# A max-pooling kernel: a short first load from one contiguous stretch, its outputs stored in the middle of the loads

## The chip, the cores and the metric

One core of one Trainium2 chip. The metric is the device time of one execution in microseconds (us); unless a range is given, a time below is a median of 4 to 9 executions. Every execution used here is marked as fast in the record, none as slow, and the granted clock was 1.0 in all.

## The reference

`x` is float32 of shape 32 x 256 x 4096 (134.2 MB). Each row of 4096 is cut into 256 windows of 16, and the output is the maximum of each window (32 x 256 x 256, 8.4 MB).

```python
for i in range(output_size):                       # 256
    start = int(i * length / output_size)
    end = int((i + 1) * length / output_size)
    result[:, :, i] = np.max(x[:, :, start:end], axis=-1)
```

## The kernel before

All 2,097,152 windows are dealt out to 128 partitions, 16,384 to each. One SBUF area of 53,200 floats per partition holds three load slots at its low end and all outputs at its high end. Outputs grow downwards, so the three slots shrink from round to round (1024, 980, 924, ... windows). Loads and stores go through one queue, issued by SyncE; VectorE reduces each slot as it lands. The outputs are stored at the end: those of the first nine loads, those of the middle loads, and the last four loads' by themselves.

```python
    sizes = []
    left = total
    while left:
        room = AREA - (total - left)
        n = min(room // (SLOTS * W + SLOTS) // ALIGN * ALIGN, MOST)   # W = 16, MOST = 1024
        for _ in range(SLOTS):                                        # SLOTS = 3
            n = min(n, left)
            if n:
                sizes.append(n)
                left -= n
    groups = [sizes[: ROUNDS_A * SLOTS], sizes[ROUNDS_A * SLOTS :]]   # ROUNDS_A = 3
    # ... (cut)
    for g, loads in enumerate(groups):
        n = sum(loads)
        xg = xw[first : first + P * n].rearrange("(p n) w -> p (n w)", p=P)
        og = ow[first : first + P * n].rearrange("(p n) -> p n", p=P)
        first += P * n
        base = low - n
        b = n
        for i, size in enumerate(loads):
            a = b - size
            at = n_loads % SLOTS * sizes[n_loads // SLOTS * SLOTS] * W
            slot = area[:, at : at + size * W]
            nc.sync.dma_start(out=slot, in_=xg[:, a * W : b * W])
            nc.vector.reduce_max(out=area[:, base + a : base + b],
                in_=slot.rearrange("p (n w) -> p n w", w=W), axis=mybir.AxisListType.X)
            n_loads += 1
            b = a
        # ... (cut: stores of a group are put on a list)
    for dst, src in stores:
        nc.sync.dma_start(out=dst, in_=src)
```

A "row" below is one partition's share of one DMA: one contiguous run in memory and one packet on one of the 16 DMA engines. With 128 partitions, each engine moves 8 rows per DMA. The rows of a load lie one group share apart: 562,176 B in the first group, 486,400 B in the second. This distance is the pitch.

## Time and profile before

Median 335.48 us (335.36 to 335.57, 6 runs).

| | before |
|---|---|
| span of the profiled execution | 333.9 us |
| DMA queue, share of 16 engines' span | 99.1% |
| moved | 142.61 MB, 427 GB/s |
| VectorE busy | 276.0 us, 83% |
| first reduce begins | 22.98 us |
| last reduce ends | 326.0 us |

Lines of the page of the kernel before: VectorE's busy time, share and instructions, then the one DMA queue with its packets, MB and share of the 16 engines' span.

```profile
span 333.9 us, 109 instructions
DVE 276.0 (83%) x19; POOL 0.2 (0%) x4
...
q1 hardware_dynamic: 3168, 142.61, 99.1%
HBM read 134.22 MB, written 8.39 MB: 427 GB/s over the span
```

The DMA engines are the limit, VectorE is not. The timeline of the kernel before shows the same. Its columns are start us, duration us, engine, source line, operation, output and input, count; in brackets stands how long the engine had idled and for what.

```profile
22.98 17.22 DVE L75 TENSOR_REDUCE area<-area 128x1024 f32<-128x16384 f32 x1 [22.98 <-DMA area<-in_x_dram]
42.33 17.22 DVE L75 TENSOR_REDUCE area<-area 128x1024 f32<-128x16384 f32 x1 [2.13 <-DMA area<-in_x_dram]
...
293.16 33.20 SPq L91 DMA_DIRECT2D out_dram<-area  x3
...
308.79 17.21 DVE L75 TENSOR_REDUCE area<-area 128x768 f32<-128x12288 f32 x2 [1.57 <-DMA area<-in_x_dram]
```

Loads of 8.39 MB land 19.35 us apart, each is reduced in 17.22 us, and the reducer waits for the next. The last reduce ends at 326.0 us; the final store is issued then, behind two earlier stores still running.

How many packets began in the first 2.75 us, by the DMA view of that window:

```profile
DMA packets 16, 1.05 MB, mean 381 GB/s; under 512 B 0, under 2 KB 0, under 8 KB 0
```

A 64 KB row takes 2.4 us, so 16 packets here are the first row of each of the 16 engines: all have started.

Two things can be worked out from the packets in the trace. A packet takes about 14 ns plus 0.0367 ns per byte, whether load or store, from 10 KB (387 ns, median) to 64 KB (2418 ns). The main exception is the very first row of each engine, which takes 2.8 to 3.8 us. And no engine idles between its first packet and its last, in this kernel.

### The profile page before, as it was taken

To read this page: it belongs to the slowest core of one execution; us is meant where nothing else is said; L and a number is where in the kernel's file an instruction comes from. 1 tells how busy PE (TensorE), PEld (TensorE's weight loads), DVE (VectorE), ACT (ScalarE), POOL (GpSimd) and SP (SyncE) were. 2 spreads that over 40 slices of the span, in tenths; PEclk is the share of its full clock that TensorE was granted. 3 is DMA by queue.
4 is the path that set the end of the run, shared out by engine and by line. 5 is a ranking of instruction groups with operands and counts; after the bars stand their busy time and mean duration, and the time that the engine had idled before them with its cause. 6 is when DMAs were issued, how large, how long until landed. Compare 5 with 4: busy or idle time off the path is not lost.

```text
span 333.9 us, 109 instructions
## 1 busy us (share of the span) xinstructions
DVE 276.0 (83%) x19; POOL 0.2 (0%) x4
## 2 busy tenths in 40 slices
DVE  0029899798979899897979897979989798988990
POOL 0000000000000000000000000000000000000000
DMA  9898989998999998999999999999999998998997
GB/s 377 377 502 377 495 385 471 392 473 376 473 443 398 474 439 383 425 453 453 446 426 433 426 426 426 426 425 469 407 419 475 395 465 389 465 436 383 448 420 311
DMA packets 3168, 142.61 MB, mean 427 GB/s; under 512 B 352, under 2 KB 352, under 8 KB 352
## 3 DMA queue, kind: packets, MB, share of 16 engines
q1 hardware_dynamic: 3168, 142.61, 99.1%
HBM read 134.22 MB, written 8.39 MB: 427 GB/s over the span
## 4 chain that ended last, share of the span: by engine, by line
DMA 63%; DVE 34%; another core or an unknown queue 1%; issue 0%; SPq 0%
DMA area<-in_x_dram 63%; DVE area L75 34%; SPq L74 0%
## 5 line engine op out<-in xcount | busy, mean ns | idle before, releaser
L75 DVE TENSOR_REDUCE area<-area 128x1024 f32<-128x16384 f32 (+6 forms) x19 | 276.0, 14525 | 50.0 <-DMA area<-in_x_dram 50.0
L108 POOL MEMSET const-bfloat16-1.0<- 128x1 bf16 x1 | 0.1, 102 | 0.0
L108 POOL MEMSET const-uint8-127<- 128x1 uint8 x1 | 0.1, 101 | 0.0
L108 POOL MEMSET const-float32-0.0<- 128x1 f32 x1 | 0.1, 100 | 0.2 <-issue 0.2
L108 POOL MEMSET const-float32-1.0<- 128x1 f32 x1 | 0.1, 99 | 0.0
## 6 DMA issues: line engine op xcount, KB each, us to landing
area<-in_x_dram SPq DMA_DIRECT2D x3, 7840.0 KB, 39.1
area<-in_x_dram SPq DMA_DIRECT2D x3, 7392.0 KB, 36.9
area<-in_x_dram SPq DMA_DIRECT2D x3, 6944.0 KB, 34.7
area<-in_x_dram SPq DMA_DIRECT2D x3, 6528.0 KB, 32.6
area<-in_x_dram SPq DMA_DIRECT2D x3, 6144.0 KB, 30.7
out_dram<-area SPq DMA_DIRECT2D x1, 4392.0 KB, 30.7
out_dram<-area SPq DMA_DIRECT2D x1, 2526.0 KB, 36.3
area<-in_x_dram SPq DMA_DIRECT2D x1, 1952.0 KB, 20.7
```

What stands on the lines that cost most here:

```text
L75: nc.vector.reduce_max(out=area[:, base + a : base + b], in_=slot.rearrange("p (n w) -> p n w", w=W), axis=mybir.AxisListType.X,)
L108: nc = _bacc.Bacc("TRN2", target_bir_lowering=False, num_devices=1)
```

## The change

The intent, as the diff shows it: VectorE should get its first data early, by a first load of 320 windows (20 KB) per partition instead of 1024 (64 KB), read as a group of its own, so from one contiguous stretch of 2.6 MB (its rows lie back to back; "packed" below). Its outputs are stored after the ninth load, on the same queue, instead of at the end. The slots are sized again from what is left. Loads stay 19; stores become 4 instead of 3.

```diff
+    FIRST = 320
+    EARLY_AT = 9
-    sizes = []
-    left = total
+    slot_sizes = [MOST]
+    rounds = [[FIRST] + [MOST] * (SLOTS - 1)]
+    left = total - sum(rounds[0])
     while left:
         room = AREA - (total - left)
         n = min(room // (SLOTS * W + SLOTS) // ALIGN * ALIGN, MOST)
+        if left <= slot_sizes[-1]:
+            n = left
 ... (cut: rounds are filled with n)
-    groups = [sizes[: ROUNDS_A * SLOTS], sizes[ROUNDS_A * SLOTS :]]
+    groups = [sizes[:1], sizes[1 : ROUNDS_A * SLOTS], sizes[ROUNDS_A * SLOTS :]]
 ... (cut)
-            at = n_loads % SLOTS * sizes[n_loads // SLOTS * SLOTS] * W
+            at = n_loads % SLOTS * slot_sizes[n_loads // SLOTS] * W
 ... (cut)
+            if n_loads == EARLY_AT:
+                dst, src = stores.pop(0)
+                nc.sync.dma_start(out=dst, in_=src)
```

More of the change, by code (lines that the diff above doesn't have):

```diff
@@ L45 @@
         n = min(room // (SLOTS * W + SLOTS) // ALIGN * ALIGN, MOST)
-        for _ in range(SLOTS):
+        if left <= slot_sizes[-1]:
+            n = left
+        slot_sizes.append(n)
+        rounds.append([])
+        while left and len(rounds[-1]) < SLOTS:
             n = min(n, left)
-            if n:
-                sizes.append(n)
-                left -= n
-    groups = [sizes[: ROUNDS_A * SLOTS], sizes[ROUNDS_A * SLOTS :]]
+            rounds[-1].append(n)
+            left -= n
+    sizes = [n for r in rounds for n in r]
+    groups = [sizes[:1], sizes[1 : ROUNDS_A * SLOTS], sizes[ROUNDS_A * SLOTS :]]
     pool = ctx.enter_context(tc.tile_pool(name="pool", bufs=1))
@@ L81 @@
             b = a
+            if n_loads == EARLY_AT:
+                dst, src = stores.pop(0)
+                nc.sync.dma_start(out=dst, in_=src)
         low = base
-        if g == 0:
+        if g < len(groups) - 1:
             stores.append((og, area[:, base : base + n]))
```

## The prediction

> **What bounds the kernel now.** The DMA engines, from first packet to last. The page gives the DMA queue 99.1% of 16 engines' span, 142.61 MB at 427 GB/s; VectorE is busy 83%. The single packets of the trace show no gap: the 16 engines start at 1.75 to 2.03 us, run back to back, and end at 331.3 to 332.5 of a 333.9 us span. So about 1.7 us lie before the stream and 1.4 us after it; the rest is bytes. VectorE's waits in the timeline (0.85 to 2.13 us before each reduce, 23.0 before the first) are slack of an engine that doesn't bind: a 128x16384 reduce takes 17.22 us, its load 19.35.
>
> The Trainium skill ("DMA: Bandwidth & Descriptors", Specifications) gives a fabric ceiling of 435 GB/s; the trace agrees: a 64 KB row takes 2418 ns on one engine, which is 434 GB/s over 16. No rate is left to win.
>
> **What the change does, costed.**
> - Bytes: the same, one queue, still 19 loads. One store more (4), so 8 rows more per engine. Packet times by row length (10,192 B 388 ns, 35,136 B 1303, 62,720 B 2315) lie on a line of 0.0367 ns per byte plus about 14 ns per row. 8 rows cost **+0.1 us**, all on the critical path. The 164 KB store (estimate 0.5 us) only moves from the end to the middle.
> - First load 20 KB instead of 64 KB per partition: it should land at about 9.5 us instead of 23.0, and the first reduce (5.4 us) end near 15 instead of 40. This slack VectorE doesn't need; loads 2 and 3 are queued anyway. Worth 0. The first row on each engine takes 2.8 to 3.8 us instead of 2.42; that start-up latency (mean 0.9) should remain.
> - Larger slots (996 instead of 980 and so on): no effect, by the line above.
> - Tail: the last load grows from 244 to 756 outputs. It should land at about 313.5 us; its reduce takes 12.7 us instead of 4.2 (the previous reduce now ends before it lands), ending near 326.3, as before (326.0). The two stores behind the last load (4.0 and 2.6 MB, 15.3 us) keep the engines busy until 328 to 329. The final store needs about 1 us from issue to first packet, so it is ready near 327.3, some 0.6 us to spare (before: 1.4). No bubble.
>
> **Sum.** 335.48 + 0.1 = 335.6 us, range 335.1 to 336.3.
>
> **What would show it.** DMA share again 99%, no packet gaps; first reduce starting near 9.7 us; VectorE's busy time still 276 us, its waits only moved (short before the first reduce, long before the second, about 1 us before the last); the last store's packets following without a gap; packet times on the same line.
>
> **What would make it wrong.** (1) Rows of the last group lie 526,080 B apart, near 512 KiB; the Trainium skill (same page, Latency and other measured facts) reports rates falling at large power-of-two row pitches. Before, pitches of 562,176 and 486,400 B show no difference; if this one does, half of the loads slow by a few per cent. (2) The early 1,280 B writes disturb the reads around them by over 0.5 us. (3) The final store comes after the queue has run dry: up to 1 us. (4) The contiguous first load shortens the start-up: up to 1 us faster.
>
> Chances: faster by over 2% 0.01, within 2% 0.96, slower by over 2% 0.03.

## The result, and the profile after

Median 336.30 us (336.12 to 336.57, 6 runs) against 335.48: by the medians 0.82 us slower. The ratio is 1.0026, 95% interval 1.0013 to 1.0039. Such a ratio is the mean time of one kernel's fast runs over that of the other's of the same rounds, so not quite the ratio of the medians quoted. By the 2% line that is "the same"; by the interval it is a small, real loss.

The page of the changed kernel, the same lines:

```profile
span 334.7 us, 110 instructions
DVE 276.0 (82%) x19; POOL 0.2 (0%) x4
...
q1 hardware_dynamic: 3312, 142.61, 98.8%
HBM read 134.22 MB, written 8.39 MB: 426 GB/s over the span
```

The timeline of the changed kernel, the first reduces, those around the early store, and the end:

```profile
10.29 5.49 DVE L84 TENSOR_REDUCE area<-area 128x320 f32<-128x5120 f32 x1 [10.29 <-DMA area<-in_x_dram]
29.61 17.22 DVE L84 TENSOR_REDUCE area<-area 128x1024 f32<-128x16384 f32 x1 [13.84 <-DMA area<-in_x_dram]
...
140.82 15.75 DVE L84 TENSOR_REDUCE area<-area 128x936 f32<-128x14976 f32 x1 [1.88 <-DMA area<-in_x_dram]
158.81 15.75 DVE L84 TENSOR_REDUCE area<-area 128x936 f32<-128x14976 f32 x1 [2.23 <-DMA area<-in_x_dram]
...
314.75 12.75 DVE L84 TENSOR_REDUCE area<-area 128x756 f32<-128x12096 f32 x1 [1.22 <-DMA area<-in_x_dram]
327.53 0.33 SPq L103 DMA_DIRECT2D out_dram<-area  x1
```

VectorE does start 12.7 us sooner, and then waits 13.84 us for the second load. Early data is worth nothing to an engine that isn't the limit. But the first load is also late: 44 KB less per row is 8 x 1657 ns = 13.26 us less per engine (by the medians, 2418 and 761 ns), so from 22.98 the first reduce should have come to 9.72 us, and it came at 10.29. That is 0.57 us of loss before anything else has happened. The DMA view of the first 2.75 us of the changed kernel:

```profile
DMA packets 15, 0.31 MB, mean 112 GB/s; under 512 B 0, under 2 KB 0, under 8 KB 0
```

15 packets, not 16: one engine has not started. The single packets show it starting at 2.95 us (in the kernel before the last engine starts at 2.03), and then taking 0.91 us beyond the line for its first row. No engine started its second row in this window, so the 15 are 15 engines.

Why one engine of 16 counts: the Trainium skill ("DMA: Bandwidth & Descriptors", section "Why a DMA increments its semaphore by 16 and not by 1") says that the participating engines finish independently and only the full count means that all data landed. This trace agrees: the first load's 16 landings come between 8.49 and 10.26 us, and the reduce begins at 10.29. And a late engine doesn't catch up, as long as every engine moves the same bytes at the same rate without a pause. Landings (median engine and last engine of the 16, in us):

| | first load: median, last, lag | last store: median, last, lag |
|---|---|---|
| before | 22.45, 22.96, 0.51 | 332.48, 332.98, 0.50 |
| changed | 8.94, 10.26, 1.32 | 332.57, 333.85, 1.28 |

The last engine ends 0.87 us later, and the program waits for that one. The median engine ends only 0.09 us later, but that is no measure of the eight rows more. It landed the first load 0.25 us sooner than its bytes alone would have put it, and it lost 0.37 us at the end: from the last store but one to the last it took 4.09 us (328.48 to 332.57), against 3.72 in e1 below, whose stores end alike. In between it had nothing to do. The DMA view from 327.9 to 328.35 us, of the changed kernel:

```profile
DMA packets 7, 0.02 MB, mean 46 GB/s; under 512 B 6, under 2 KB 6, under 8 KB 6
```

and of e1:

```profile
DMA packets 17, 0.16 MB, mean 348 GB/s; under 512 B 5, under 2 KB 5, under 8 KB 5
```

The packets under 512 B are 4 B each, one per engine and DMA. So one row of data began in this window, against 12 in e1; for a moment as few as 4 of the 16 engines were moving anything. Most engines had run dry before the last store, issued at 327.53, reached them: its first rows began at 328.36. The late engine was still busy, so the program's end did not move by this.

### The profile page after: what moved, and what is told of

It reads as the page before. It is cut to its first block, busy times and chain, and to the rows that moved or that the text cites. A ratio compares the mean times of both kernels' runs of the same rounds, so it can differ in the third digit from the quotient of the medians.

```text
span 334.7 us, 110 instructions
## 1 busy us (share of the span) xinstructions
DVE 276.0 (82%) x19; POOL 0.2 (0%) x4
## 3 DMA queue, kind: packets, MB, share of 16 engines
q1 hardware_dynamic: 3312, 142.61, 98.8%
## 4 chain that ended last, share of the span: by engine, by line
DMA 65%; DVE 31%; another core or an unknown queue 0%; SPq 0%; issue 0%; DVEq 0%
DMA area<-in_x_dram 65%; DVE area L84 31%; SPq L83 0%; DVEq L84 0%
## 5 line engine op out<-in xcount | busy, mean ns | idle before, releaser
L84 DVE TENSOR_REDUCE area<-area 128x996 f32<-128x15936 f32 (+7 forms) x19 | 276.0, 14525 | 51.5 <-DMA area<-in_x_dram 51.5
```

The lines of the kernel that those rows point to most:

```text
L84: nc.vector.reduce_max(out=area[:, base + a : base + b], in_=slot.rearrange("p (n w) -> p n w", w=W), axis=mybir.AxisListType.X,)
```

## The experiments

To compare loads of different row lengths, one number is read from each timeline, the **lead**: the start of the first reduce, less the time that eight rows of S bytes take on the line, 8 x (14 ns + 0.0367 ns x S). This time is 19.34 us for 64 KB and 6.12 us for 20 KB (with the line's two numbers unrounded), so the lead is 3.64 us before and 4.17 changed. It contains everything that the latest engine loses at the start. The expectations below speak instead of when the latest engine "begins its second row" with the row's length taken off: the same from the packets, about 0.35 us smaller (the rest is from the last packet's end to the reduce).

The theories: START (the first load makes one engine late), STORE (the writes in the middle cost more than their bytes), and of START two forms, short rows or a packed source.

All 16 runs gave a correct result. Times are medians; "before" is the kernel before on the same chip.

| run | first load | lead us | time us | before |
|---|---|---|---|---|
| kernel before | 64 KB rows, pitch 549 KB | 3.64 | 335.48 | |
| changed | 20 KB packed, early store | 4.17 | 336.30 | 335.48 |
| e12_changed_again | the same | 4.06 | 336.28 | 335.61 |
| e1_store_late | 20 KB packed | 3.92 | 336.06 | 335.53 |
| e8_issue_later | 20 KB packed | 4.20 | 336.19 | 335.52 |
| e15_packed_20k_end | 20 KB packed, end of x | 3.90 | 335.86 | 335.49 |
| e2_short_strided | 20 KB rows, pitch 510 KB | 3.42 | 335.52 | 335.53 |
| e5_pitch_84k | 20 KB rows, pitch 84 KB | 3.36 | 335.32 | 335.52 |
| e16_pitch_40k | 20 KB rows, pitch 40 KB | 3.33 | 335.38 | 335.49 |
| e9_contig_16k | 16 KB packed | 3.43 | 335.63 | 335.61 |
| e10_contig_24k | 24 KB packed | 3.74 | 335.66 | 335.61 |
| e13_packed_28k | 28 KB packed | 3.22 | 335.47 | 335.49 |
| e6_contig_32k | 32 KB packed | 3.11 | 335.43 | 335.52 |
| e11_32k_early | 32 KB packed, early store | 3.23 | 335.42 | 335.61 |
| e14_packed_40k | 40 KB packed | 4.00 | 335.85 | 335.49 |
| e3_long_contig | 64 KB packed | 3.34 | 335.34 | 335.53 |

Two more (e4 and e7) follow in the text. Every run with a lead of 3.9 us or more lost 0.35 us or more; no other lost more than 0.1. The experiments ran on four chips (e1 to e4, e5 to e8, e9 to e12, e13 to e16), and each of the four saw a lead of 3.9 us or more, so it is not the fault of one chip.

### e1: the early store moved to the end

```diff
-            if n_loads == EARLY_AT:
-                dst, src = stores.pop(0)
-                nc.sync.dma_start(out=dst, in_=src)
```

> The changed kernel without its early store: the first load's 164 KB are stored after the last load instead. In the changed kernel the last of the 16 DMA engines lands the first load 1.3 us behind the median engine (0.5 us in the kernel before), stays there, and falls 0.3 us further back around the early store. Theory START (the first load causes the lag): first load again lands at 10.0 to 10.4 us with a lag of 1.0 to 1.4 us, and the time is 335.9 to 336.2. Theory STORE (the writes in the middle cause the loss): the time falls to 335.4 to 335.6. If the two add up as the trace suggests: 336.0.

336.06 us (335.67 to 336.38), ratio 1.0015 (1.0003 to 1.0028). The lag on the first load is 1.10 us. Both theories get a part, START the larger. (How large STORE's part is rests on the traces: the intervals of this run and of the changed kernel overlap.) Its timeline, to be set against that of the changed kernel:

```profile
10.04 5.49 DVE L84 TENSOR_REDUCE area<-area 128x320 f32<-128x5120 f32 x1 [10.04 <-DMA area<-in_x_dram]
...
140.59 15.75 DVE L84 TENSOR_REDUCE area<-area 128x936 f32<-128x14976 f32 x1 [1.87 <-DMA area<-in_x_dram]
158.29 15.75 DVE L84 TENSOR_REDUCE area<-area 128x936 f32<-128x14976 f32 x1 [1.95 <-DMA area<-in_x_dram]
```

Without the store the ninth load lands 17.70 us after the eighth; with it, 17.99 us, although the store's own packets run after that load's.

### e2: the same short rows, not packed

```diff
-    groups = [sizes[:1], sizes[1 : ROUNDS_A * SLOTS], sizes[ROUNDS_A * SLOTS :]]
+    groups = [sizes[: ROUNDS_A * SLOTS], sizes[ROUNDS_A * SLOTS :]]
```
(on top of e1)

> The same slots and the same short first load of 20 KB per partition, but its rows are 502 KB + 20 KB apart in x, as part of the first group (no contiguous stretch of its own, no early store, three stores as before). If the contiguous source makes an engine start late: the lag of the last engine behind the median on the first load is 0.4 to 0.6 us and the time 335.2 to 335.6. If the shortness of the rows does: lag 1.0 to 1.4 us and 335.9 to 336.2, like the run without the early store.

335.52 us, ratio 1.000; lag 0.58. The first reduce comes half a microsecond sooner than in e1, and all 16 engines have started by 2.75 us (the last at 2.71, so the count at 2.75 is a coarse sign; the lead is the measure):

```profile
9.54 5.49 DVE L84 TENSOR_REDUCE area<-area 128x320 f32<-128x5120 f32 x1 [9.54 <-DMA area<-in_x_dram]
```

```profile
DMA packets 16, 0.33 MB, mean 119 GB/s; under 512 B 0, under 2 KB 0, under 8 KB 0
```

No run of e2 (335.45 to 335.64) was as slow as the fastest of e1 (335.67). So it is not the shortness by itself. (The pitch here is 522,496 B, 510 KB; the expectations round it differently.)

### e3: 64 KB rows, packed

The kernel before, with the first of its nine loads made a group of its own and stored at the end (four stores).

```diff
-    groups = [sizes[: ROUNDS_A * SLOTS], sizes[ROUNDS_A * SLOTS :]]
+    groups = [sizes[:1], sizes[1 : ROUNDS_A * SLOTS], sizes[ROUNDS_A * SLOTS :]]
-        if g == 0:
+        if g < len(groups) - 1:
```

> The kernel before with its slots, but the first load (64 KB per partition) comes from one contiguous stretch, stored at the end. If the contiguous source is the cause: lag of the last engine on the first load 1.0 to 1.4 us, time 335.9 to 336.3. If the shortness is: lag 0.5, time 335.5 to 335.7 (one store more).

335.34 us, ratio 0.9993 (0.998 to 1.0005); lag 0.40. So it is not packing by itself either: of these three first loads only the one that is both short and packed has the lag. I had not expected that.

### e4: an early store alone

The kernel before, storing 320 of the first load's outputs after the ninth load.

```diff
+            if n_loads == EARLY_AT:
+                nc.sync.dma_start(out=og[:, n - FIRST :], in_=area[:, base + n - FIRST : base + n])
...
-            stores.append((og, area[:, base : base + n]))
+            stores.append((og[:, : n - FIRST], area[:, base : base + n - FIRST]))
```

> The kernel before plus an early store alone: 320 of the first load's outputs per partition (the same 128 rows of 1,280 B, 164 KB) stored after the ninth load, the rest at the end. If the early store costs what the trace of the changed kernel shows (0.3 us on the last engine, 0.1 for eight rows more): 335.8 to 335.9, with the last engine's lag growing by 0.3 us at the store. If it costs only its rows: 335.5 to 335.6.

335.61 us against 335.53, ratio 1.0002 (0.9988 to 1.0016); lead 3.60. The last engine's lag is 0.39 us on the load before the store and 0.39 on the ninth. In this trace the store costs its rows and no more, here where no engine is far behind; the time's interval alone would not exclude 0.3 us.

### e5: 20 KB rows 84 KB apart

`groups = [sizes[:2], sizes[2 : 9], sizes[9 :]]` on top of e1: the first two loads share a group.

> Changed kernel with its stores at the end, but the first two loads share a group: the 20 KB rows of the first load lie 84 KB apart instead of back to back. So far the latest engine begins its second row of the first load's stretch (start plus what the first row takes beyond its bytes) at: kernel before 3.29 us, contiguous 20 KB 3.63 and 3.86, strided 20 KB (522 KB apart) 3.09, contiguous 64 KB 2.97. If packing the short rows tightly in the memory is the cause: here 3.1 and 335.4 to 335.6. If any pitch well below 500 KB does it: 3.6 or more, 335.9 to 336.2.

335.32 us, ratio 0.9994 (0.9979 to 1.0009), lead 3.36. So a pitch well below 500 KB is not the cause: at this row length the straggler comes with packing.

### e6: 32 KB rows, packed

`FIRST = 512` on top of e1.

> Changed kernel with stores at the end and a first load of 32 KB instead of 20 KB per partition, contiguous. If the lag comes from rows that are short and packed: it lies between those of 20 KB and 64 KB (latest engine 3.2 to 3.5 us, time 335.5 to 335.8). If 20 KB is an unlucky size alone: 3.0, 335.3 to 335.5.

335.43 us, ratio 0.9997; lead 3.11, with the smallest lag of all, 0.16 us. That answers to "20 KB is an unlucky size", not to a smooth fall with length.

### e7: the packed 20 KB load in second place

`rounds = [[MOST, FIRST] + ...]` and a packed group for each of the first two loads.

> The contiguous 20 KB load comes second, behind a contiguous 64 KB load. If short contiguous reads as such slow one engine (a conflict in the memory): its lag behind the median grows by 0.5 us or more from load 1 to load 2, time 335.9 or more. If it is an effect of the start of the stream: no row of the second load takes longer than its line (765 ns), the lag stays near 0.4, time 335.4 to 335.6 (two stores more than before, 0.2 us).

335.39 us, ratio 0.9997. The lag is 0.47 us on the first load and 0.43 on the second. Reading the packed 20 KB rows slows nobody once the stream runs: the loss belongs to the start.

### e8: nothing else issued while the engines start

```diff
+            if n_loads == 1:
+                nc.vector.memset(slot[:, :2048], 0.0)
             nc.sync.dma_start(out=slot, in_=xg[:, a * W : b * W])
```
(on top of e1; the second load must wait for the memset)

> Changed kernel with stores at the end; a small VectorE memset of the second slot makes the second load's issue wait until some 1 us or more later, so nothing else is being issued while the first load's engines start (the first load lasts until 9 us, so no gap). If the issue of the second and third load within 0.5 us of the first makes an engine start late when rows are short: all engines start their first row by 2.1 us, lag 0.4, time 335.4 to 335.6. If not: one engine late as before, 335.9 to 336.2.

336.19 us, ratio 1.0018 (1.0001 to 1.0034), lead 4.20. The second load's issue moved from 1.16 to 3.02 us, and still one engine was missing at 2.75 us:

```profile
DMA packets 15, 0.31 MB, mean 112 GB/s; under 512 B 0, under 2 KB 0, under 8 KB 0
```

```profile
1.22 1.76 DVE L84 MEMSET area<- 128x2048 f32 x1 [1.22 <-PEq L119]
10.32 5.49 DVE L86 TENSOR_REDUCE area<-area 128x320 f32<-128x5120 f32 x1 [7.33 <-DMA area<-in_x_dram]
```

My guess that the issues of the next two loads hold the engine up is refuted.

### e9 and e10: 16 and 24 KB rows, packed

`FIRST = 256` and `FIRST = 384` on top of e1 (the first gives one load more).

> As the changed kernel with stores at the end, first load contiguous with 16 KB rows (one load more in all, 0.1 us). So far the packed 20 KB rows alone gave a straggling engine (beginning its second row at 3.6 to 3.9 us) in three runs of three; 32 and 64 KB packed and 20 KB at pitches of 84 and 522 KB gave 2.8 to 3.1. If every packed first load of short rows does it: 3.5 or more, 336.0 to 336.4. If 20 KB is special: 3.1 or less, 335.4 to 335.7.

> As the run of 32 KB, with 24 KB rows. If shortness below some length does it: latest engine at 3.3 to 3.9 us, time 335.7 to 336.2. If 20 KB is special: 3.1 or less, 335.3 to 335.6.

16 KB: 335.63 against 335.61, lead 3.43, lag 0.22: no straggler. 24 KB: 335.66, lead 3.74, lag 0.77: in between, and not separable from "before" by its time (ratio 1.0004, 0.999 to 1.0017).

### e11: the changed kernel, first load 32 KB

`FIRST = 512` in the changed kernel, the early store kept.

> The changed kernel entire, early store included, but with a first load of 32 KB per partition. If the row size of the packed first load is the cause of nearly all the loss: 335.4 to 335.6. If the early store costs 0.3 us by itself: 335.7 to 335.9, with the lag of the last engine growing by 0.3 us at load 8.

335.42 us, ratio 0.9996 (0.9983 to 1.0008), against 336.28 for the changed kernel; the slowest run here (335.64) was faster than the fastest there (335.97). One constant takes the whole loss away (the slots are sized again with it). With no straggler the early store costs nothing beyond its rows either; the eighth and ninth load are reduced 17.62 us apart, the usual distance:

```profile
143.16 15.69 DVE L84 TENSOR_REDUCE area<-area 128x932 f32<-128x14912 f32 x1 [1.86 <-DMA area<-in_x_dram]
160.78 15.69 DVE L84 TENSOR_REDUCE area<-area 128x932 f32<-128x14912 f32 x1 [1.94 <-DMA area<-in_x_dram]
```

### e12: the changed kernel again

No edit.

> The changed kernel once more, for a second trace of it: straggler again at 3.6 us or later at the start (if not, one bad trace misled me), 336.1 to 336.5; and whether the 0.3 us that the straggler lost around the early store is there again. If it isn't, that part of the explanation falls.

336.28 us (335.97 to 336.56), ratio 1.002 (1.0006 to 1.0034). The straggler is there again, starting at 3.18 us by the packets, and so is its loss at the store:

```profile
DMA packets 15, 0.31 MB, mean 112 GB/s; under 512 B 0, under 2 KB 0, under 8 KB 0
```

```profile
140.72 15.75 DVE L84 TENSOR_REDUCE area<-area 128x936 f32<-128x14976 f32 x1 [1.87 <-DMA area<-in_x_dram]
158.71 15.75 DVE L84 TENSOR_REDUCE area<-area 128x936 f32<-128x14976 f32 x1 [2.23 <-DMA area<-in_x_dram]
```

17.99 us again. The last engine's lag grows by 0.24 us at the ninth load (1.17 to 1.41), and by 0.30 in the first trace of the changed kernel (1.32 to 1.62).

### e13 to e16: which packed rows

e13 and e14 set `FIRST` to 448 and 640 on top of e1. e15 reads the packed 20 KB rows from the end of `x` and shifts all else forward. e16 makes the first two loads 320 windows each and lets them share a group, so the first rows lie 40 KB apart.

> Packed first load with 28 KB rows, stores at the end. If it goes by length alone, falling from 20 KB on: latest engine begins its second row at 3.0 to 3.3 us (counted from the span's start, the length of a row taken off), 335.4 to 335.7. If pitches that are no power of two are bad: 3.5 or more, 335.9 to 336.2.

> Packed first load with 40 KB rows, stores at the end. By length: 2.8 to 3.1 and 335.3 to 335.6. If pitches that are no power of two, or multiples of 20 KB, are bad: 3.5 or more, 335.9 to 336.2.

> Packed 20 KB rows as in the changed kernel with its stores at the end, but the stretch lies at the end of x and everything else at its beginning. If the lag comes with rows of 20 KB back to back wherever they lie: one engine at 3.5 or later, 335.9 to 336.2. If it belongs to the place in memory: 3.1 or less, 335.4 to 335.6.

> The first 20 KB rows at a pitch of 40 KB (the second load takes the other halves). If the density or the 20 KB pitch is the cause: latest engine at 3.1 or less, 335.4 to 335.7 (one load more than the run without the early store, 0.1 us). If short rows from any region of a few MB do it: 3.5 or more, 336.0 to 336.3.

28 KB: 335.47, lead 3.22, no straggler. 40 KB: 335.85 (335.67 to 335.94), ratio 1.0011 (0.9996 to 1.0026), lead 4.00, one engine starting at 2.93 us. From the end of x: 335.86, ratio 1.0013 (0.9998 to 1.0028), lead 3.90; here no engine is missing at 2.75 us, the latest one starts at 2.50 us and then takes 1.12 us beyond the line for its first row. Pitch of 40 KB: 335.38, lead 3.33. The two intervals just reach 1, so the times alone don't carry these two losses; the leads, 0.57 to 0.78 us above those of e13 and e16, do. Timelines of e14 and e16:

```profile
16.13 10.82 DVE L84 TENSOR_REDUCE area<-area 128x640 f32<-128x10240 f32 x1 [16.13 <-DMA area<-in_x_dram]
```

```profile
9.45 5.49 DVE L84 TENSOR_REDUCE area<-area 128x320 f32<-128x5120 f32 x1 [9.45 <-DMA area<-in_x_dram]
```

The place in x is not the cause, and length alone is ruled out (20 and 40 KB lose, 16, 28, 32 and 64 don't). In e14 and e16 the rows begin at the same distance from each other, 40 KB, and only the one whose rows touch has a straggler. **Open:** why packed rows of 20 and 40 KB, and 24 KB in part, make one engine late. The traces show that an engine starts late or is slow in its first row, not what it waits for, and the packets kept carry no engine number, so whether it is always the same engine isn't known either. That multiples of 20 KB are bad would fit too; 60 KB was not tried. Most of these variants have one trace each.

## Why the prediction was right or wrong

Right in its class (within 2%) and its sign, wrong in size: +0.1 us forecast, +0.8 measured, at the very upper end of the range. No risk named a slower start, so that the range reaches so far is luck.

- **The limit: right.** DMA share 98.8%, VectorE 276.0 us as before, no gap between packets until the last store (see the tail). The Trainium skill's ceiling of 435 GB/s ("DMA: Bandwidth & Descriptors", Specifications) again fits: a 64 KB row takes 2418 ns.
- **Eight rows more, 0.1 us: not contradicted, and too small to be seen in the times.** The store's rows of 1,280 B took 55 ns each, some 8 ns beyond their bytes at 0.0367 ns. In e4 the time rose by 0.08 us, within its interval. That the median engine ends 0.09 us later is no confirmation, as shown above.
- **"That start-up latency (mean 0.9) should remain": the step that failed.** It put the change's start-up at the old one's and so entered 0 in the sum. I took the mean over 16 engines, and the mean hardly matters. The latest engine decides, and its start-up grew by 0.53 us (lead 3.64 to 4.17; 0.57 with the median row of 761 ns instead of the line's 765), while the median engine's first landing came 0.25 us sooner than its bytes alone would have put it (8.94 against 22.45 - 13.26 = 9.19). Risk 4 had the right place, the start-up with a contiguous source, with the wrong sign. e2 and e11 show that this first load is the cause: the same short rows not packed, or packed rows of 32 KB, cost nothing. Why it makes one engine late stays open.
- **"The 164 KB store only moves": off by 0.3 us, and only here.** In both traces of the changed kernel the ninth load came 0.29 us late; in e4 and e11, with the same kind of store and no straggler, it didn't. The loss sits in one row: the straggler's own last row of that load took 357 ns longer than the line, 398 in e12, and it ran while the other engines were already storing. Last rows of other engines were slow too (up to 336 ns), but so they were in e4 and e11 (up to 246 and 291), where the latest engine's took only 59 and 116. A reading that fits is that a row of a load is slowed while other engines write, and that the straggler's row, which ran longest among such writes, lost most. That reading is argued; the extra loss itself is read from the traces. Risk 2 put it at over 0.5 us in general, which e4 refutes.
- **The tail: right in shape, the margin more than used up.** I put the last load at 313.5 us, the last reduce's end at 326.3. The straggler made that 314.66 and 327.5, and the final store was issued at 327.53 instead of about 326.3; its first rows began at 328.36 where I had put 327.3. So "no bubble" failed for most engines, and risk 3 came: in both traces of the changed kernel, and in no other, they idled before the last store (the median engine 0.37 us, 0.1 in e12). It cost nothing only because the last engine, already late, saw no gap: its last store landed 3.71 us after the previous one, as in e1.
- **The sum.** On the last engine: start 0.57 (10.29 against 9.72), eight rows 0.1, store 0.3; together 0.97, measured 0.87 at the last landing. The remaining -0.1 us is not accounted for. Against e1, which has the same rows, it closes better: start 0.25, store 0.3, measured 0.52 at the last landing.
- **Risk 1, the row pitch of 526,080 B: didn't come.** The Trainium skill (same page, "Latency and other measured facts") reports losses at large power-of-two pitches. In the changed kernel, 49,920 B rows at this pitch, 1,792 B above 512 KiB, took 1848 ns (median); the line of the kernel before gives 1845.

Nothing beat the kernel before by more than the intervals allow: the best, e5 and e3, are 0.2 us faster with intervals that contain 1. What remains to be won there is, as an estimate, the start's lag in its trace, about half a microsecond in 335.

## What to carry to other kernels

When the DMA engines are busy from the first packet to the last, giving compute its first data sooner was worth nothing here; look instead at the slowest of the 16 engines, because every load, and the end of the program, waits for that one, and here a lag from the start was carried to the end. Compare the engines' landings, not their mean, and count the packets that began in the first microseconds: one missing engine explained most of this loss. Treat the first load's shape as something to measure: a change from 20 KB to 32 KB packed rows was worth 0.8 us. The count alone is not enough (e15 had all 16 engines running and a straggler all the same), so take the start of the first reduce less its bytes as well. And when the last engine is late, look whether the others have run out of work: their idling hides in a share of 98.8%.

## What the Trainium skill lacked or had wrong

- "DMA: Bandwidth & Descriptors": nothing on how far apart the 16 engines start a stream. In the kernel before they start 1.75 to 2.03 us into the span; in other runs without a straggler the last one started as late as 2.71 (e2). With packed first rows of 20 KB one started at 2.94 to 3.56 in four traces of five. The first row takes up to 1.6 us more than its bytes (e10). A lag at the start is not made up (0.51 us on the first load, 0.50 on the last store of the kernel before).
- The same page, "Latency and other measured facts": the row-pitch entry gives +4 KiB as enough to restore the full rate and +192 B as not enough, at a pitch of 4 MiB, and nothing in between. 526,080 B (512 KiB + 1,792) showed no loss here: 1848 ns a row against 1845.
- The same page, "Bandwidth": it gives about 10.5 ns per packet as a floor for small packets, for DMAs issued from GpSimd. It gives no time per long row on top of the bytes; by the line above that was about 14 ns here, for rows of 10 to 64 KB on the SyncE queue.
- The same page, "Latency and other measured facts": about 0.6 us to the first byte, without saying from when. It holds if counted from the end of the issuing instruction (1.11 to 1.75 us, 0.63); from its start it is 1.0 us.
- No page says that packed first rows of one length can cost more than those of another: leads of 3.9 to 4.2 us for 20 and 40 KB, 3.7 for 24 KB, 3.1 to 3.4 for 16, 28, 32 and 64 KB.
